# Rotary tables in 64 rows of 1 KB through ScalarE's DMA ring, and the last slab stored whole

## The chip, the cores and the metric

One core of a Trainium2 chip. The metric is the device time of one execution in microseconds (us); lower is better. A program on one core has no second die to compare with, so a run counts as fast unless it lies over 1.5% above the fastest of its kernel. Ratios and their 95% intervals are of the fast runs alone against the kernel before; they are not quite the ratios of the medians that stand beside them. A median and its range cover all runs, unless slow ones are named. "Span" is the length of the profiled execution, which is about 1.8 us shorter than the time measured for the same run.

## The reference

```python
batch, seq, dim, num_heads = 16, 512, 1024, 16        # head_dim 64, half_dim 32
x = x.reshape(batch, seq, num_heads, head_dim)        # float32
x1, x2 = x[..., :half_dim], x[..., half_dim:]
cos = cos[None, :, None, :]; sin = sin[None, :, None, :]   # each (seq, 32), float32
rotated = np.concatenate([x1 * cos - x2 * sin, x1 * sin + x2 * cos], axis=-1)
```

33.55 MB are read, 33.55 MB are written, and two tables of 64 KB, cos and sin, are shared by all batches and heads.

## The kernel before

Eight slabs of 4 MB (two batches each, one row of 32 KB per partition) go through five buffers. SyncE issues the loads, ScalarE the stores. The transfers that one of them issues stand in its own ring, a queue that sixteen DMA engines empty; the profile calls SyncE's ring q1 and ScalarE's q10. ScalarE casts a slab to bf16, VectorE multiplies twice and adds once, ScalarE casts back into the slab.

```python
load(0)
table = {}
raw = singles.tile([P, 2 * TR * half], f32, tag="raw")
for i, src in enumerate((cos, sin)):                       # 128 rows of 512 B each
    table[i] = nc.gpsimd.dma_start(out=view(raw, ...), in_=bass.AP(..., ap=[[TR * half, P], [1, TR * half]]))
for s in range(1, slots):                                  # loads 1 to 4 wait for the cos table
    tc.add_manual_dep(load(s).ins, table[0].ins.name, ...)
# ... four affine_selects build 0/1/-1 matrices "pick"; one cast raw -> tab1 (bf16)
# ... eight matmuls spread the table rows to the partitions of a slab: acc
tab = singles.tile([P, 2 * rpp * hd], bf16, tag="tab")
nc.vector.tensor_copy(out=tab, in_=acc)
# ... slabs 0, 6 and 7 in two half passes, the others in one
    back = nc.scalar.copy(out=xs, in_=xu)
    if s == nslabs - 1:                                    # last slab: each half stored by itself
        # ... second half's cast ordered behind the first half's issue
        part = nc.scalar.dma_start(out=dram(out_flat, s, r * dim, n * dim), in_=xs)
    elif r + n == rpp:
        nc.scalar.dma_start(out=dram(out_flat, s), in_=slab[s])
        if s + slots < nslabs:
            load(s + slots)
```

Each transfer issued by SyncE or ScalarE takes the next of eight semaphores in turn, and waits until the previous user of that semaphore has landed. At the end SyncE checks all semaphores, two by two, in a fixed order.

## Time and profile before

| | before |
|---|---|
| time, median of the runs beside the changed kernel | 162.49 us (162.31 to 162.63, 4 runs) |
| span of the profiled run | 160.43 us |
| first packet of the DMA engines; end of the last | 1.76; 158.97 us |
| load 0, sin table, load 1 landed | 13.40; 10.97; 23.11 us |
| store 0 issued; last store issued | 37.20; 145.13 us |

One "packet" is what a DMA engine moves in one turn: here a whole 32 KB row in 1.213 us. After the rows of a transfer each engine sends one more packet of 4 bytes, which counts its semaphore up (a semaphore packet). "Landed" is the time at which the semaphore has its full count. Packets and landings are read from the trace's records; the lines of the profile that carry the argument are in the prediction.

### The profile page before, as it was taken

The page shows a single profiled execution, that of the slowest core. Times are in us where ns is not written, and L with a number is a line of the kernel's source. Part 1 is how long each engine was busy: PE and PEld are TensorE (multiplying, and loading weights), DVE is VectorE, ACT ScalarE, POOL GpSimd, SP SyncE. Part 2 cuts the span into 40 slices and gives each one's busy share as a digit, 9 for nine tenths or more (in the row PEclk, how much of TensorE's full clock was granted, in tenths as well). Part 3 has the DMA queues.
Part 4 walks back from the last instruction along what each step waited for, and adds up shares of the span by engine and source line. Part 5 has one row for each costly group of instructions (what it writes and reads, how often), then busy time and mean ns, then how long its engine had stood idle before and what let it go on. Part 6 is the DMA issues. An engine that isn't in the chain of part 4 may idle for free.

```text
span 160.4 us, 169 instructions
## 1 busy us (share of the span) xinstructions
PE 1.0 (1%) x8; PEld 0.8 (1%) x8; DVE 108.5 (68%) x34; ACT 113.5 (71%) x23; POOL 3.4 (2%) x12
## 2 busy tenths in 40 slices
PE   0011000000000000000000000000000000000000
PEld 0010000000000000000000000000000000000000
DVE  0003799999989979997996099939649599920000
ACT  3006939998998999899907997099995999471000
POOL 7000000000000000000000000000000000000000
DMA  7999999999999999999999999999999999999994
GB/s 229 441 409 400 474 433 392 449 466 392 392 392 449 466 392 425 490 392 409 490 409 409 482 417 392 490 425 392 458 458 392 433 482 392 417 490 400 400 437 208
DMA packets 2512, 67.24 MB, mean 419 GB/s; under 512 B 304, under 2 KB 304, under 8 KB 336
## 3 DMA queue, kind: packets, MB, share of 16 engines
q1 hardware_dynamic: 1152, 33.55, 49.4%
q10 hardware_dynamic: 1296, 33.56, 48.5%
q0 software_dynamic: 64, 0.13, 0.2%
HBM read 33.69 MB, written 33.55 MB: 419 GB/s over the span
## 4 chain that ended last, share of the span: by engine, by line
DMA 59%; ACT 17%; issue 9%; DVE 4%; SPq 0%; POOLq 0%
DMA slab<-in_x_dram 40%; DMA out_dram<-slab 15%; ACT slab L146 11%; ACT xb L119 6%; DMA raw<-in_cos_dram 4%; DVE xb L143 1%; DVE xb L140 1%; DVE slab L140 1%; SPq L62 0%; POOLq L177 0%
## 5 line engine op out<-in xcount | busy, mean ns | idle before, releaser
L119 ACT CAST xb<-slab 128x4096 bf16<-128x4096 f32 (+1 forms) x11 | 56.6, 5155 | 27.4 <-DMA slab<-in_x_dram 26.1
L146 ACT CAST slab<-xb 128x4096 f32<-128x4096 bf16 (+1 forms) x11 | 56.6, 5153 | 3.4 <-DVE xb L143 3.4
L140 DVE TENSOR_TENSOR slab<-xb,tab 128x4096 bf16<-128x4096 bf16 (+1 forms) x11 | 35.9, 3260 | 19.7 <-ACT xb L119 19.6
L143 DVE TENSOR_TENSOR xb<-xb,slab 128x4096 bf16<-128x4096 bf16 (+1 forms) x11 | 35.9, 3261 | 0.3
L140 DVE TENSOR_TENSOR xb<-xb,tab 128x4096 bf16<-128x4096 bf16 (+1 forms) x11 | 35.9, 3260 | 0.3
L110 DVE CAST tab<-acc 128x1024 bf16<-128x1024 f32 x1 | 1.2, 1225 | 12.6 <-PE acc L104 12.6
L119 ACT ACT_TABLE_LOAD x1 | 1.3, 1283 | 0.7 <-PEq L177 0.7
L104 PE MATMUL acc<-tab,pick 128*128 128x128 bf16 x8 | 1.0, 305 | 11.6 <-POOL tab L98 11.6
L92 POOL TENSOR_SCALAR_AFFINE_SELECT pick<-pick 128x128 bf16<-128x128 bf16 x4 | 1.0, 289 | 0.1
L104 PEld LDWEIGHTS <-pick 128*128 128x128 bf16 x8 | 0.8, 136 | 11.4 <-issue 8.1
L73 POOL DMA_DIRECT2D raw<-in_cos_dram x1 | 0.7, 677 | 0.8 <-POOLq L177 0.8
L98 POOL CAST tab<-raw 128x256 bf16<-128x256 f32 x1 | 0.4, 398 | 7.0 <-DMA raw<-in_sin_dram 7.0
L89 POOL MEMSET pick<- 128x512 bf16 x1 | 0.5, 544 | 0.0
L73 POOL DMA_DIRECT2D raw<-in_sin_dram x1 | 0.5, 537 | 0.0
L177 POOL MEMSET const-float32-0.0<- 128x1 f32 x1 | 0.1, 99 | 0.2 <-issue 0.2
L177 POOL MEMSET const-bfloat16-1.0<- 128x1 bf16 x1 | 0.1, 102 | 0.0
L177 POOL MEMSET const-uint8-127<- 128x1 uint8 x1 | 0.1, 102 | 0.0
L177 POOL MEMSET const-float32-1.0<- 128x1 f32 x1 | 0.1, 99 | 0.0
## 6 DMA issues: line engine op xcount, KB each, us to landing
slab<-in_x_dram SPq DMA_DIRECT2D x8, 4096.0 KB, 24.6
out_dram<-slab ACTq DMA_DIRECT2D x7, 4096.0 KB, 27.8
out_dram<-slab ACTq DMA_DIRECT2D x2, 2048.0 KB, 15.3
raw<-in_cos_dram POOLq DMA_DIRECT2D x1, 64.0 KB, 7.1
raw<-in_sin_dram POOLq DMA_DIRECT2D x1, 64.0 KB, 9.1
```

The costliest lines, as they stand in the source:

```text
L73: table[i] = nc.gpsimd.dma_start(out=view(raw, i * TR * half, (1, TR * half)), in_=bass.AP(tensor=src.tensor, offset=src.offset, ap=[[TR * ...
L89: nc.gpsimd.memset(pick, 0.0)
L92: nc.gpsimd.affine_select(out=part, in_=part, compare_op=mybir.AluOpType.not_equal, fill=1.0 if g < G else -1.0, base=-(g % G), pattern=[[ ...
L98: nc.gpsimd.tensor_copy(out=tab1, in_=raw)
L104: nc.tensor.matmul(view(acc, (i * rpp + g * TR) * hd + h * half, (hd, TR), (1, half)), view(pick, (i * h * G + g) * P, (1, P)), view(tab1, ...
L110: nc.vector.tensor_copy(out=tab, in_=acc)
L119: nc.scalar.copy(out=view(xb[s], r * dim, (1, n * dim)), in_=view(slab[s], r * dim, (1, n * dim)))
L140: nc.vector.tensor_mul(out=t, in0=xu, in1=view(tab, a + r * hd, (hd, n), (0, nh), (1, hd)))
L143: nc.vector.tensor_add(out=xu, in0=xu, in1=view(t2, half, (hd, n * nh), (-half, 2), (1, half)))
L146: back = nc.scalar.copy(out=xs, in_=xu)
L177: nc = _bacc.Bacc("TRN2", target_bir_lowering=False, num_devices=1)
```

## The change

Its intent: get the tables off GpSimd's software queue and drop the loads' wait for them, halve the matmuls and selections, and save one store and its ordering.

```diff
-    raw = singles.tile([P, 2 * TR * half], f32, tag="raw")
-    ... two nc.gpsimd.dma_start of 128 rows of 512 B
-    for s in range(1, slots):
-        tc.add_manual_dep(load(s).ins, table[0].ins.name, ...)
+    cos_sb = singles.tile([SP, TW], f32, tag="cos_sb")        # SP = 64 rows of TW = 256 floats
+    sin_sb = singles.tile([SP, TW], f32, tag="sin_sb")
+    for t, src in ((cos_sb, cos), (sin_sb, sin)):
+        nc.scalar.dma_start(out=t, in_=bass.AP(..., ap=[[TW, SP], [1, TW]]))
+    for s in range(1, slots):
+        load(s)
     ... two affine_selects on 64 partitions instead of four on 128; two casts instead of one
-            for g in range(G):                                # eight matmuls of 128 columns
+            nc.tensor.matmul(...)                             # four of 256
-        back = nc.scalar.copy(out=xs, in_=xu)
-        if s == nslabs - 1:
-            ... part = nc.scalar.dma_start(... half ...)
-        elif r + n == rpp:
+        nc.scalar.copy(out=xs, in_=xu)
+        if r + n == rpp:
             nc.scalar.dma_start(out=dram(out_flat, s), in_=slab[s])
```

More of the change, by code (lines that the diff above doesn't have):

```diff
@@ L65 @@
     load(0)
-    TR = seq // P
-    G = rpp // TR
-    table = {}
-    raw = singles.tile([P, 2 * TR * half], f32, tag="raw")
-    for i, src in enumerate((cos, sin)):
-        table[i] = nc.gpsimd.dma_start(out=view(raw, i * TR * half, (1, TR * half)), in_=bass.AP(
-            tensor=src.tensor, offset=src.offset,
-            ap=[[TR * half, P], [1, TR * half]]))
-    for s in range(1, slots):
-        tc.add_manual_dep(
-            load(s).ins, table[0].ins.name,
-            mybir.DependencyInfo(mybir.DependencyClass.Sync,
-                                 mybir.DependencyReason.DATA),
-            reason="issue")
-    pick = singles.tile([P, 2 * G * P], bf16, tag="pick")
+    cos_sb = singles.tile([SP, TW], f32, tag="cos_sb")
+    sin_sb = singles.tile([SP, TW], f32, tag="sin_sb")
+    for t, src in ((cos_sb, cos), (sin_sb, sin)):
+        nc.scalar.dma_start(out=t, in_=bass.AP(
+            tensor=src.tensor, offset=src.offset, ap=[[TW, SP], [1, TW]]))
+    for s in range(1, slots):
+        load(s)
+    pick = singles.tile([SP, 2 * P], bf16, tag="pick")
     nc.gpsimd.memset(pick, 0.0)
-    for g in range(2 * G):
+    for g in range(2):
         part = view(pick, g * P, (SP, P // SP), (1, SP))
@@ L93 @@
             out=part, in_=part, compare_op=mybir.AluOpType.not_equal,
-            fill=1.0 if g < G else -1.0, base=-(g % G),
-            pattern=[[0, P // SP], [-G, SP]], channel_multiplier=1)
-    tab1 = singles.tile([P, 2 * TR * half], bf16, tag="tab1")
-    nc.gpsimd.tensor_copy(out=tab1, in_=raw)
+            fill=1.0 - 2.0 * g, base=0, pattern=[[0, P // SP], [-1, SP]],
+            channel_multiplier=1)
+    tab1 = singles.tile([SP, 2 * TW], bf16, tag="tab1")
+    for i, t in enumerate((cos_sb, sin_sb)):
+        nc.gpsimd.tensor_copy(out=view(tab1, i * TW, (1, TW)), in_=t)
     acc = psum.tile([P, 2 * rpp * hd], f32, tag="acc")
@@ L102 @@
         for h in range(2):
-            for g in range(G):
-                nc.tensor.matmul(
-                    view(acc, (i * rpp + g * TR) * hd + h * half, (hd, TR), (1, half)),
-                    view(pick, (i * h * G + g) * P, (1, P)),
-                    view(tab1, i * TR * half, (half, TR), (1, half)),
-                    start=True, stop=True)
+            nc.tensor.matmul(
+                view(acc, i * rpp * hd + h * half, (hd, rpp), (1, half)),
+                view(pick, i * h * P, (1, P)),
+                view(tab1, i * TW, (half, rpp), (1, half)),
+                start=True, stop=True)
     tab = singles.tile([P, 2 * rpp * hd], bf16, tag="tab")
@@ L144 @@
             out=xu, in0=xu, in1=view(t2, half, (hd, n * nh), (-half, 2), (1, half)))
-        back = nc.scalar.copy(out=xs, in_=xu)
-        if s == nslabs - 1:
-            if r > 0:
-                tc.add_manual_dep(
-                    back.ins, part.ins.name,
-                    mybir.DependencyInfo(mybir.DependencyClass.NoSync,
-                                         mybir.DependencyReason.DATA),
-                    reason="issue")
-            part = nc.scalar.dma_start(
-                out=dram(out_flat, s, r * dim, n * dim), in_=xs)
-        elif r + n == rpp:
+        nc.scalar.copy(out=xs, in_=xu)
+        if r + n == rpp:
             nc.scalar.dma_start(out=dram(out_flat, s), in_=slab[s])
```

## The prediction

> **What bounds the kernel now.** I read the page first: the busy slices and the DMA part.
>
> ```profile
> span 160.4 us, 169 instructions
> ...
> DVE  0003799999989979997996099939649599920000
> ACT  3006939998998999899907997099995999471000
> ...
> DMA  7999999999999999999999999999999999999994
> ...
> q1 hardware_dynamic: 1152, 33.55, 49.4%
> q10 hardware_dynamic: 1296, 33.56, 48.5%
> q0 software_dynamic: 64, 0.13, 0.2%
> ```
>
> VectorE and ScalarE have holes throughout; the DMA row has none between its first and its last slice. The three queues are SyncE's loads (q1), ScalarE's stores (q10) and GpSimd's two tables (q0). Their packets fill 49.4 + 48.5 + 0.2 = 98.1% of sixteen engines' span, 157.4 of 160.4 us, so at most 3.0 us of the span have an engine without a packet. The trace's packet records place them: the engines' first packets start between 1.76 and 2.60 us, the last ends at 158.97 us, and in between no engine pauses for more than 0.1 us. One packet is a 32 KB row and takes 1.213 us in the median; an engine has 8 loads and 8 stores of 8 rows each, 128 rows, 128 x 1.213 = 155.3 us. This is the bound: it can be beaten only by fewer bytes, faster packets, an earlier first packet or a shorter tail.
>
> Next the chain of waits in order of time, because it seems to say something else:
>
> ```profile
> 1.24 7.10 DMA raw<-in_cos_dram
> 8.33 0.02 issue
> 8.35 14.76 DMA slab<-in_x_dram
> 23.11 0.02 issue
> 23.14 3.00 ACT xb L119
> ```
>
> The end is followed back through the wait of loads 1 to 4 for the cos table: 7.10 us that the change removes. The reader might book them as a gain. But load 0 lands only at 13.40 us, so SyncE's ring still held rows of load 0 when the other loads were issued at 8.35. Busy time by stretches shows it (columns: stretch, length, busy PE, PEld, DVE, ACT, POOL, clock, DMA share, GB/s):
>
> ```profile
> 2.00:8.35 6.35, 0.00 (x0) 0.10 (x1) 0.00 (x0) 0.01 (x1) 2.01 (x6) 1.00 0.86 361
> 8.35:13.40 5.05, 1.01 (x8) 0.74 (x7) 0.80 (x1) 0.00 (x0) 0.40 (x1) 1.00 1.00 428
> ```
>
> The share in a stretch counts a packet where it starts; the 0.86 is the first row of each engine, which began just before 2.00 and took 1.5 to 2.3 us, not idleness. At 8.35 nothing had run dry: share 1.00 to 13.40.
>
> Last the timeline of the start and of the end, for the slack of the compute chain:
>
> ```profile
> 11.10 0.40 POOL L98 CAST tab<-raw 128x256 bf16<-128x256 f32 x1 [7.02 <-DMA raw<-in_sin_dram]
> ...
> 12.60 1.23 DVE L110 CAST tab<-acc 128x1024 bf16<-128x1024 f32 x1 [12.60 <-PE acc L104]
> 13.43 7.11 ACT L119 CAST xb<-slab 128x4096 bf16<-128x4096 f32 x2 [11.41 <-DMA slab<-in_x_dram]
> 17.06 2.29 DVE L140 TENSOR_TENSOR slab<-xb,tab 128x4096 bf16<-128x4096 bf16 x1 [3.24 <-ACT xb L119]
> ...
> 28.32 2.29 DVE L143 TENSOR_TENSOR xb<-xb,slab 128x4096 bf16<-128x4096 bf16 x1
> 30.06 7.11 ACT L146 CAST slab<-xb 128x4096 f32<-128x4096 bf16 x2
> ```
>
> And of the end:
>
> ```profile
> 138.12 0.34 ACTq L155 DMA_DIRECT2D out_dram<-slab  x1
> ...
> 145.13 0.34 ACTq L155 DMA_DIRECT2D out_dram<-slab  x1
> ```
>
> The finished table stands at 12.60 + 1.23 = 13.83 us, yet VectorE starts at 17.06: it waits for ScalarE's cast of the first half slab, which waits for load 0. And the last store is issued at 145.13, while the span ends at 160.4: over 15 us in which only DMA works.
>
> **What the Trainium skill says.** "DMA: Bandwidth & Descriptors", section "Queues, rings and completion order", says that each DMA engine goes round the queues that have work and changes only at packet boundaries. This trace agrees: while q0 had table packets, each engine put one 1.213 us row of q1 between two turns of q0. The same page, section "Issuing engines are not separate DMA queues", says that the issuing engine does not matter to bandwidth, only to its sequencer's time; here an issue took 0.34 us on ScalarE, 0.33 to 0.46 on SyncE, and 0.68 and 0.54 on GpSimd. Section "Where 436 GB/s comes from" derives a ceiling of 435.2 GB/s; 16 rows of 32,768 B in 1.213 us are 432 GB/s, so faster packets are not to be expected. "SBUF — State Buffer", section "Door 1: The DMA port swizzle", says that a tile on partitions 0 to 63 reaches only half of the write ports; here that concerns two tables of 64 KB among 33.69 MB read, so I leave it out, and no run so far shows it.
>
> **The change part by part.**
>
> (1) Wait of loads 1 to 4 on the table: removed. They will be queued behind load 0 by about 0.74 + 5 x 0.4 = 2.7 us instead of 10.1 us. Rows within the ring stay in order, load 0 first. Gain: 0, since the ring was never empty.
>
> (2) Tables by ScalarE's ring. Before, q0 had 64 packets: per engine and table one of 4,096 B (eight 512 B pieces, 159 ns) and one semaphore packet (9 ns), so 2 x 168 ns = 0.34 us of an engine. After, 64 rows of 1 KB over 16 engines are 4 rows per engine and table. If ScalarE's ring sends each as its own packet, as it does with 32 KB rows, that is 8 rows and 2 semaphores per engine; I estimate 50 ns for a row (a quarter of 159 ns and something for a packet): 8 x 50 + 2 x 9 = 0.42 us. Cost of the DMA engines: +0.1 us.
>
> (3) The tables come later. Ten turns per engine instead of four, a q1 row between each. When does a new ring get its first turn? q0's first packet started at 6.0 us, four to five us after its issue; the first store, issued at 37.20, got its first packet at 42.24, 5.0 us later, behind about four rows of q1. I choose the same for the tables: issue at 0.75, first turn at about 6.0. From there nine more turns have nine packets of q1 between them; one is load 0's semaphore packet, so eight rows: 6.0 + 8 x 1.213 + 0.5 = 16.2 us on the typical engine, 16.5 on the last, against 10.97 before. cos needs five turns: 6.0 + 4 x 1.27 = about 11.1. If the table rows go in with the first rows of load 0 instead, sin lands near 14.
>
> (4) From sin's landing to the table: the cast of 64x256 as long as that of 128x256, 0.40; of four matmuls (256 columns instead of 128, half as many as before) only the two of sin are still to come, about 0.5; eviction of the same 128x1024, 1.23; semaphores 0.2. 16.5 + 2.3 = 18.8 us. VectorE's first multiply moves from 17.06 to 18.8, by 1.7 us. Before, it was hidden behind load 0 with 3.2 us to spare; now it is the table that VectorE waits for.
>
> (5) What those 1.7 us cost. Slab 0's last addition ends at 28.32 + 2.29 = 30.61; ScalarE wants it at 30.06 + 3.55 = 33.6, because its cast of slab 1 waits for load 1 (23.11). Slack 3.0 us, so store 0 is still issued at 37.2. Slab 1's last addition (39.45 + 4.43 = 43.88 in the timeline) has 0.66 us before ScalarE wants it (44.54), so store 1 goes out 1.0 us late, at 52.6; but ScalarE's ring is busy with store 0 until 61.25, and store 1 has 9 us of slack. ScalarE has 4.88 us idle before 85.14, which absorb the rest. DMA: 0.
>
> (6) GpSimd: the memset and two selections instead of four, on 64 partitions, and no DMA issue. All done by 4 us then as now, waiting for sin. 0.
>
> (7) The last store whole. Its first half was issued at 138.12; now all goes at 145.13. At that time ScalarE's ring holds store 6, whose rows end at 148.74 us in the packet records. Load 0 shows that an empty ring starts 1.0 us after the issue, so the whole store is in the ring at about 146.2, 2.5 us before it is needed. Then 8 rows of 1.213 = 9.70 us against 16 half rows of 0.611 = 9.78. -0.1 us.
>
> Sum: 0 + 0.1 + 0 - 0.1 = 0 us.
>
> **The rivals.** First: the 7.10 us of the chain are real and come off, 155.5 us. For it speaks only the chain; against it the full DMA row and the 1.00 share between 8.35 and 13.40. Hardly possible, since 155.3 us of rows remain, with 1.8 us before them.
> Second: the late table delays the first store and the whole chain behind it, by 1.7 us or more: 164.3. For it: VectorE's wait does change hands. Against it: the slack of 3.0 us, and five slabs of buffers: with all loads queued, DMA has read work to about 52 us without a single store. If ScalarE's ring had to stand behind all five loads the tables would come at about 50 us, and VectorE's start and with it store 0 would move from 37.2 to some 74, and about 20 us without DMA would follow; but the first store began 5.0 us after its issue with q1 still full, and then took turns one to one.
> Third: a hole before the last store. It opens only if the last cast slips by over 2.5 us, through a later load 7 (now 123.85); then each further us costs one: 163 to 165.
> Fourth: a small gain. On q10's first use, at 40.3 to 42.6 us, each engine's row of q1 took 1.6 to 2.1 instead of 1.213 us, 0.65 us more. If that is the price of a ring's first use, the tables now pay it inside the slow first rows, and up to 0.6 us come off: 161.9.
>
> **Range and chances.** The three runs before lie within 0.23 us. The sum is 0, with the fourth rival a little likelier than the third: 162.4 us, 161.6 to 163.3 for 8 in 10. Within 2% means 159.3 to 165.8: 0.96. Faster 0.01, as the rows leave no room; slower 0.03, for tables stuck behind the loads.
>
> **What would show it.** Right: DMA shares of the queues near 98% again; loads 1 to 4 issued by 3 us without moving load 1's landing from 23.1; sin landing at 14 to 17, VectorE's first wait ended by the table; store 0 still at 37.2; last issue at 145 with 15 us to the end; GpSimd's queue gone. Wrong: a slice of the DMA row below 9 inside, sin landing after 20, store 0 after 38, or rows slower than 1.213 us.

## More of the kernel before

One view that the prediction did not use becomes important later: SyncE's own waits (what waited, on whom, us in total, times, longest).

```profile
SPq L62 <- DMA out_dram<-slab: 87.8, 3, 51.1
SPq L191 <- DMA out_dram<-slab: 35.4, 1, 35.4
...
SPq L62 <- DMA raw<-in_cos_dram: 7.2, 1, 7.2
```

L62 is the load: three loads wait for stores to free a buffer, and load 1 waits 7.2 us for the cos table. L191 is the end of the program. There a single check waits for a store, the last one; no later check has anything left to wait for, but each still takes its time.

## The result, and the profile after

The changed kernel took 161.99 us (161.92 to 162.55, 4 runs) against 162.49; the ratio is 0.9979, 95% interval 0.9960 to 0.9998. It is the same within 2%, with a gain of 0.03 to 0.65 us that just clears the noise. The spans of its four runs are 160.2, 160.1, 160.8 and 160.2 us.

The page of the changed kernel, to be laid beside the lines in the prediction:

```profile
span 160.2 us, 157 instructions
...
DMA  7999999999999999999999999999999999999993
...
q1 hardware_dynamic: 1152, 33.55, 49.3%
q10 hardware_dynamic: 1312, 33.69, 48.8%
```

The DMA row is as full as before, the queues fill 49.3 + 48.8 = 98.1% of the span as before, and GpSimd's queue is gone. That is why a change with so many parts moves so little; e2_tables and e3_free below take the parts alone.

The start of its timeline, and its last store (start, length, engine and line, what):

```profile
0.74 2.50 SPq L62 DMA_DIRECT2D slab<-in_x_dram  x5
0.75 0.54 ACTq L71 DMA_DIRECT2D cos_sb<-in_cos_dram  x1
...
1.32 0.61 ACTq L71 DMA_DIRECT2D sin_sb<-in_sin_dram  x1
...
17.59 0.39 POOL L90 CAST tab<-sin_sb 64x256 bf16<-64x256 f32 x1 [4.91 <-DMA sin_sb<-in_sin_dram]
...
18.65 1.22 DVE L101 CAST tab<-acc 128x1024 bf16<-128x1024 f32 x1 [18.65 <-PE acc L95]
19.97 2.29 DVE L131 TENSOR_TENSOR slab<-xb,tab 128x4096 bf16<-128x4096 bf16 x1
...
31.23 2.29 DVE L134 TENSOR_TENSOR xb<-xb,slab 128x4096 bf16<-128x4096 bf16 x1
...
37.70 0.35 ACTq L139 DMA_DIRECT2D out_dram<-slab  x1
...
144.28 0.34 ACTq L139 DMA_DIRECT2D out_dram<-slab  x1
```

All five loads are issued by 3.2 us instead of 10.1, yet load 1 landed at 23.61 us, half a us later than before. The tables come later, not earlier: sin landed at 17.54 us against 10.97. VectorE starts at 19.97 instead of 17.06, with no idle time between the table and its first multiply, so the table is now what it waits for. Its last addition for slab 0 ends at 33.52, still before ScalarE wants it (30.56 + 3.55 = 34.11), so store 0 goes out at 37.70; the 0.5 us against before are load 1's.

The chain of waits (start, length, what) looks quite different:

```profile
0.75 11.49 DMA cos_sb<-in_cos_dram
...
19.97 2.30 DVE slab L131
...
68.21 30.49 DMA out_dram<-slab
98.70 0.02 SPq L62
98.72 0.04 issue
98.76 24.18 DMA slab<-in_x_dram
```

Before, it ran through the cos table, load 1, store 0, load 5 and load 7; now it runs through the table and VectorE's first slabs to store 2 and load 7. A new 11.49 us wait for a table stands on it, and the time did not grow. A chain shows one path back from the last instruction that ended on an engine; here, with the DMA engines full all the time, the waits on it were exchanged without any effect on the end.

### The profile page after: what moved, and what is told of

It is laid out like the page before. It is cut to its first block, busy times and chain, and to the rows that moved or that the text cites. A ratio compares the mean times of both kernels' runs of the same rounds, so it can differ in the third digit from the quotient of the medians.

```text
span 160.2 us, 157 instructions
## 1 busy us (share of the span) xinstructions
PE 1.2 (1%) x4; PEld 0.5 (0%) x4; DVE 108.4 (68%) x34; ACT 113.6 (71%) x23; POOL 1.8 (1%) x9
## 3 DMA queue, kind: packets, MB, share of 16 engines
q1 hardware_dynamic: 1152, 33.55, 49.3%
q10 hardware_dynamic: 1312, 33.69, 48.8%
## 4 chain that ended last, share of the span: by engine, by line
DMA 41%; ACT 21%; DVE 20%; issue 6%; PE 0%; POOLq 0%; POOL 0%; ACTq 0%; DVEq 0%; SPq 0%
DMA out_dram<-slab 19%; DMA slab<-in_x_dram 15%; ACT slab L137 13%; ACT xb L110 8%; DMA cos_sb<-in_cos_dram 7%; DVE xb L131 7%; DVE slab L131 7%; DVE xb L134 6%; DVE tab L101 1%; PE acc L95 0%; POOLq L172 0%; POOL tab L90 0%; ACTq L139 0%; DVEq L131 0%; SPq L62 0%
## 5 line engine op out<-in xcount | busy, mean ns | idle before, releaser
L95 PE MATMUL acc<-tab,pick 64*128 64x256 bf16 x4 | 1.2, 392 | 17.5 <-POOL tab L90 17.5
L83 POOL TENSOR_SCALAR_AFFINE_SELECT pick<-pick 64x128 bf16<-64x128 bf16 x2 | 0.5, 287 | 0.1
L95 PEld LDWEIGHTS <-pick 64*128 64x128 bf16 x4 | 0.5, 113 | 17.7 <-issue 16.2
## 6 DMA issues: line engine op xcount, KB each, us to landing
sin_sb<-in_sin_dram ACTq DMA_DIRECT2D x1, 64.0 KB, 16.2
```

The source lines that it names most:

```text
L83: nc.gpsimd.affine_select(out=part, in_=part, compare_op=mybir.AluOpType.not_equal, fill=1.0 - 2.0 * g, base=0, pattern=[[0, P // SP], [-1 ...
L95: nc.tensor.matmul(view(acc, i * rpp * hd + h * half, (hd, rpp), (1, half)), view(pick, i * h * P, (1, P)), view(tab1, i * TW, (half, rpp) ...
```

## The experiments

Twelve kernels ran, all correct. The theory at the start: only DMA time counts, and the small gain is a row of the loads that is no longer stretched. In the kernel before, the last row of each engine ahead of the first store (at 40.3 us) took 1.56 to 2.13 instead of 1.213 us, 0.66 us per engine; in the changed kernel that is gone, while 80 rows beside the table packets took 1.27 to 1.36 us, 0.42 us per engine. The rivals: the gain is the tail's, or the removed wait's.

### Each part by itself

**e1_whole**: only the last store whole.

```diff
 kernel before
-        if s == nslabs - 1:
-            ... each half stored by itself
-        elif r + n == rpp:
+        if r + n == rpp:
```

> The kernel before with only the last store whole. My theory (the store ring is never empty before the end, so how the last slab is cut doesn't matter): the same time as before, within 0.2 us (162.3 to 162.6), the last packet ends near 158.9 us, and the rows of q1 at 40 us are stretched by 0.65 us as before. Rival (the 0.5 us gained come from the tail: fewer packets and no second issue): near 162.0, and the last packet ends 0.3 us or more earlier.

162.13 us (161.96 to 162.35, 5 runs) beside 162.39 of before: ratio 0.9982 (0.9970 to 0.9995). My theory fails: this part alone brings a gain of 0.29 us, about as large as the whole change's 0.34. The stretched rows at 40 us are still there (0.85 us per engine). But the rival's second half fails too: the last packet does not end earlier (159.15 us against 158.97). What this trace gains over before lies after its last packet: 1.20 us to the end of the span against 1.45.

**e2_tables**: the other parts without that one.

```diff
 changed kernel
-        if r + n == rpp:
+        if s == nslabs - 1:
+            ... each half stored by itself
+        elif r + n == rpp:
```

> The changed kernel with the last store in two halves again, so only the tables by ScalarE's ring and the loads without a wait. My theory (the gain is the stretched row at the first use of ScalarE's ring, 0.65 us, less 0.4 us that rows lose beside the table packets): the whole of the gain, near 162.0 to 162.2, no stretched row at 40 us, 80 or so stretched rows between 8 and 16 us. Rival (the tail): 162.5.

162.30 us (162.25 to 162.77, 5 runs), ratio 1.0000 (0.9988 to 1.0012). Tables and free loads bring nothing measurable, although the stretch at 40 us shrank to 0.12 us per engine in this trace and 96 rows beside the tables lengthened as expected. The stretched row is not the gain.

**e3_free**: the loads without their wait, tables still by GpSimd.

```diff
 kernel before
-        tc.add_manual_dep(load(s).ins, table[0].ins.name, ...)
+        load(s)
```

> The kernel before, its loads 1 to 4 not waiting for the cos table any more, tables still by GpSimd. My theory: nothing, 162.4 to 162.6, because the load ring was not empty when they were issued. Rival (the 7.10 us of the chain of waits are real): 155.5; a weaker one (earlier descriptors fill the ring better): 162.0.

162.45 us (162.38 to 164.37, 6 runs), ratio 1.0022 (0.9989 to 1.0056). Of the 7.10 us on the chain of waits the interval leaves at most 0.2 us to gain.

**e4_warm**: an early use of ScalarE's ring.

```diff
 kernel before
     load(0)
+    warm = singles.tile([16, 128], f32, tag="warm")
+    nc.scalar.dma_start(out=warm, in_=bass.AP(tensor=cos.tensor, offset=cos.offset, ap=[[128, 16], [1, 128]]))
```

> The kernel before with one 8 KB load more, 16 rows of 512 B, in ScalarE's ring right after load 0; nobody reads it. My theory (each engine's row of q1 at 40 us is stretched because ScalarE's ring is used for the first time, whatever it moves): no stretched row at 40 us, at most a few short ones near 6 us, busy time per engine down by 0.5 to 0.65 us, time 161.8 to 162.0, so the extra load makes the kernel faster. Rival (the stretch belongs to the first store, the turn from reading to writing): 162.5, the stretch still there at 40 us.

162.51 us (162.38 to 162.72, 5 runs), ratio 1.0006 (0.9994 to 1.0018), and the stretch stands at 40 us as before (0.84 us per engine). "A ring's first use costs it" is refuted. What causes the stretch stays open: it appeared in all traces with GpSimd's tables, was small or absent in most of those with the tables in ScalarE's ring, and still stood, 0.56 us, in one of these (e10_rows below).

### What happens after the last packet

The records of SyncE's last instructions show it. After the last landing SyncE finishes its checks, 0.062 us apart, and then all engines meet twice and the semaphores are cleared. Semaphores are dealt out in turn, so the number of transfers decides where the last store's semaphore stands in the order of checks. SyncE's waits in e1_whole:

```profile
SPq L181 <- DMA out_dram<-slab: 36.0, 4, 9.6
```

Before, one long check caught the last store first, and four more checks came after its landing. Here four checks wait for the last four stores one by one, 9.6 us each at the longest, and the last store's is the last: nothing is left to check when it lands. Four checks of 0.062 are 0.25 us; from the last landing to the end it is 0.88 us here against 1.11. To test this I shifted the turn with transfers that nobody reads.

**e12_one**: whole store as in e1_whole, and one 64-byte load more.

```diff
 e1_whole
+    nop = singles.tile([1, 16], f32, tag="nop0", name="nop")
+    nc.sync.dma_start(out=nop, in_=bass.AP(tensor=cos.tensor, offset=cos.offset, ap=[[16, 1], [1, 16]]))
```

> The kernel before with the last store whole (which alone took 0.3 us off) and one 64-byte load more, which shifts the semaphores back, so that the last store's is again followed by four checks. My theory: from the last landing to the end 1.1 us again instead of 0.88, and the gain of the whole store shrinks to its packets, 0.05 us: 162.3 to 162.45, as before. Rival: the gain stays, 162.1.

162.34 us (162.19 to 162.66, 5 runs), ratio 0.9998 (0.9985 to 1.0010). The gain is gone, as the theory has it (though its interval overlaps that of e1_whole), and SyncE's waits have their old form:

```profile
SPq L186 <- DMA out_dram<-slab: 54.8, 1, 54.8
```

**e11_seven**: the reverse, two halves and seven loads more.

```diff
 kernel before
+    for k in range(7):                       # behind load 4, in SyncE's ring
+        nop = singles.tile([1, 16], f32, tag=f"nop{k}", name="nop")
+        nc.sync.dma_start(out=nop, ...)      # 64 bytes, as above
```

> The kernel before, its last store in two halves, with seven 64-byte loads more in SyncE's ring behind load 4; nobody reads them. They shift the round of eight DMA semaphores, so that the last store's semaphore is the last that SyncE checks at the end, not the first of the remaining five pairs. My theory (0.25 us of the gain is this order of checks, which the whole store happens to change): from the last landing to the end of the span 0.88 us instead of 1.11, time 0.15 to 0.25 us below before, about 162.2, although it does more. Rival (the whole store itself, its larger packets, brings the gain): not faster than before, 162.4 to 162.7.

166.10 us (165.53 to 167.41, 6 runs), ratio 1.023 (1.0201 to 1.0258). The edit broke something else. The small loads queued behind load 4 and landed only at about 62 us; store 1 needed the semaphore of one of them and went out at 62.35 us instead of 51.59, and the DMA engines ran dry (1.4 us per engine of holes, and 1.9 us of longer rows after 60 us). From the last packet's end to the end of the span it took 1.23 us, as expected, but the time says nothing about it.

**e14_six**: the same for the changed kernel, six loads.

```diff
 changed kernel
+    for k in range(6):                       # behind load 4, in SyncE's ring
+        ... the same 64-byte load
```

> The changed kernel with six 64-byte loads in SyncE's ring behind load 4, to bring the last store's semaphore to the last check there too. My theory: from the last landing to the end 0.8 to 0.9 us instead of 1.00, time 0.1 to 0.2 us below the changed kernel: 161.8 to 161.9, faster than both. Rival: no gain over the changed kernel, 162.0 to 162.2.

164.84 us (163.81 to 164.91 in 4 fast runs; two slow ones at 167.13 and 167.44), ratio 1.0123 (1.0101 to 1.0145). A related fault: the six loads move store 1 on to the semaphore of load 4 itself, which landed at 65.44 us, so store 1 went out at 65.52 us (in the trace, which fell into a slow run, so I take no more from it).

**e15_first7**: seven small loads where they hold up no store. (They do hold up the issue of loads 2 to 4, to 13.4 us and later; load 2 landed at 32.79 us, before at 32.83.)

```diff
 kernel before
+    for k in range(7):                       # the first of all, in ScalarE's ring
+        nop = singles.tile([1, 16], f32, tag=f"nop{k}", name="nop")
+        nc.scalar.dma_start(out=nop, ...)
     load(0)
```

> The kernel before, its last store in two halves, with seven 64-byte loads more, this time the first of all in ScalarE's ring, where no later transfer has to wait long for their semaphores (the earlier version held up store 1, issued at 62.35 instead of 51.6 us). The last half's semaphore is again the last that SyncE checks. My theory: from the last packet's end to the end of the span 1.20 to 1.25 us instead of 1.45, so 0.1 to 0.2 us faster than before with the same two halves: 162.2 to 162.4. Rival (the whole store's larger packets gain the 0.3 us): not faster, 162.4 to 162.7.

162.18 us (162.14 to 162.31, 4 runs) beside 162.40, ratio 0.9988 (0.9973 to 1.0002). With the two halves kept and seven transfers more, it is 0.2 us faster, in size as expected; but the interval includes 1, so the time alone does not show it. SyncE's waits:

```profile
SPq L196 <- DMA out_dram<-slab: 36.1, 5, 9.6
```

Five waits for stores, one after the other, so again the last check is the last store's. The traces of fast runs that bear on it, from the records:

| kernel | last store | checks after its landing | last packet's end, span | difference, us |
|---|---|---|---|---|
| before | halves | 4 | 158.97, 160.43 | 1.45 |
| e12_one | whole | 4 | 158.97, 160.42 | 1.45 |
| e1_whole | whole | 0 | 159.15, 160.35 | 1.20 |
| e15_first7 | halves | 0 | 159.15, 160.38 | 1.22 |
| e2_tables | halves | 4 | 159.60, 160.98 | 1.38 |
| changed kernel | whole | 3 | 158.87, 160.21 | 1.34 |

In the first four rows the difference follows the number of checks and not the form of the store: four checks are 0.23 us with the halves and 0.24 us with the whole store. The other fast traces fit: e4_warm, with one transfer more than before, has 5 checks and 1.50 us; e3_free 4 and 1.45; e11_seven none and 1.23; e7_late1, e9_tail and e10_rows 3 and 1.33 to 1.34. Clearing the semaphores took 0.139 us with GpSimd's tables and 0.096 to 0.098 us without; with the changed kernel's one check less, that is most of what sets the last two rows apart from the first. So the traces show what the order of checks costs. That it makes up the timed gain of e1_whole (0.29 us, 0.08 to 0.49 by its interval) fits, but it is at the edge of the noise.

### How late the tables and the last store may come

**e7_late1**: the tables behind load 1.

```diff
 changed kernel
-    for t, src in ((cos_sb, cos), (sin_sb, sin)):
-        nc.scalar.dma_start(...)
-    for s in range(1, slots):
-        load(s)
+    load(1)
+    for t, src in ((cos_sb, cos), (sin_sb, sin)):
+        nc.sync.dma_start(...)
+    for s in range(2, slots):
+        load(s)
```

> The changed kernel with its tables in SyncE's ring behind load 1 instead of in ScalarE's, so they land at about 24 us instead of 17.5, and VectorE starts at about 26.4 instead of 20.0. Theory of the prediction (a late table costs nothing while loads are left): store 0 goes out at about 43.6 us instead of 37.7, the DMA engines stay full or lose about 1 us at 61 us when load 5 waits for store 0; 162 to 163. Rival (a late table moves everything behind it one to one): 168. It also shows what stretches a row of q1 at 40 us in the kernels with GpSimd's tables: if this kernel, with neither GpSimd's ring nor an early use of ScalarE's, has the stretch at its first store, an early and longer use of ScalarE's ring removes it; if not, GpSimd's ring causes it.

163.49 us (162.06 to 163.50 in 3 fast runs; a slow one at 165.00), ratio 1.0034 (1.0001 to 1.0067). Its timeline:

```profile
25.01 1.23 DVE L104 CAST tab<-acc 128x1024 bf16<-128x1024 f32 x1 [25.01 <-PE acc L98]
26.34 4.49 DVE L134 TENSOR_TENSOR slab<-xb,tab 128x4096 bf16<-128x4096 bf16 x2
...
44.67 0.38 ACTq L142 DMA_DIRECT2D out_dram<-slab  x1
```

VectorE starts 6.4 us later than in the changed kernel, store 0 goes out 7.0 us later, and the ratio puts the kernel 0.5 us above before: nowhere near one to one. It is not free either. SyncE's ring started no row between 54.6 and 66.6 us, because load 5 waits for store 0. The engines still had stores (holes of only 0.09 us each), but rows after 60 us lengthened by 1.13 us per engine. There was no stretch before the first store here, with neither GpSimd's ring nor an early use of ScalarE's, so an early use is not needed to remove it. But right behind the table packets, at 22.1 to 22.7 us, sixteen rows took 1.56 to 1.84 us, 0.43 us per engine: a stretch of the same kind in another place.

**e10_rows**: the old layout in the new ring.

```diff
 kernel before, last store whole, loads without their wait
-        table[i] = nc.gpsimd.dma_start(...)  # 128 rows of 512 B
+        table[i] = nc.scalar.dma_start(...)
```

> The changed kernel's ring and whole store, with the layout of before: each table in 128 rows of 512 B on 128 partitions, all through ScalarE's ring. It measures what the 64 rows of 1 KB do. My theory (one row is one packet and one turn beside a row of q1): 18 turns per engine instead of 10, sin lands at about 28 us instead of 17.5, VectorE starts at about 30.5, store 0 goes out at about 47.6; the loads end at about 52 us, so a hole of 1 to 3 us opens there or at 62 us: 163 to 165. Rival (the packets are packed as in GpSimd's queue, or the layout doesn't matter): sin by 18 us, 162.0.

163.40 us (162.65 to 164.81, 4 runs), ratio 1.0071 (1.0033 to 1.0108).

```profile
23.47 0.40 POOL L94 CAST tab<-raw 128x256 bf16<-128x256 f32 x1 [21.12 <-DMA raw<-in_sin_dram]
...
24.97 1.23 DVE L106 CAST tab<-acc 128x1024 bf16<-128x1024 f32 x1 [24.97 <-PE acc L100]
```

The records have 256 packets of 512 B, one for each row, so packets are not packed together in this ring, and sin landed at 23.34 us instead of 17.54. It came sooner than the 28 us I had worked out. Its first packet started at 3.57 us, not at 6, which is half of that; and the turns lay about 1.23 us apart, two of them only 0.28, instead of the 1.3 of the changed kernel. No row beside these packets lengthened, so the lengthening in the changed kernel goes with the new layout of 64 partitions and 1 KB rows; which of the two does it, no run shows. Store 0 went out at 43.57 us. The 64 rows of 1 KB thus matter: without them the new ring costs over a us.

**e16_first6**: the shifted checks for the changed kernel, better placed.

```diff
 changed kernel
+    for k in range(5):                       # the first of all, in ScalarE's ring
+        ... nc.scalar.dma_start(out=nop, ...)
     load(0)
     ...
+    nc.sync.dma_start(out=nop, ...)          # one more, behind load 4
```

> The changed kernel with six 64-byte loads more, five the first of all in ScalarE's ring and one in SyncE's behind load 4, to bring the last store's semaphore to the last check. The tables are issued about 1.8 us later, and should land at 19 to 20 us. My theory: from the last packet's end to the end 1.15 to 1.2 us instead of 1.34, store 0 at most 2 us later without effect, time 0.1 to 0.2 us under the changed kernel's: 161.8 to 162.0. Rival: no gain, 162.0 to 162.3.

165.83 us (165.01 to 166.50 in 5 fast runs; a slow one at 167.57), ratio 1.0206 (1.0182 to 1.0230). A miss of my own model: each small load is two packets (64 bytes and a semaphore) on one engine, each packet takes a turn beside a row of 1.213 us, so five of them are ten turns ahead of the tables on that engine. In its trace (a slow run) sin landed at 26.04 us, 8.5 us later, and store 0 was issued at 45.75. The step from the last packet's end to the end of the span was 1.16 us, but the kernel lost far more than it could gain: at 60 to 70 us alone the trace has 2.0 us of holes per engine.

**e9_tail**: the last two slabs in one pass each, so that the compute chain ends later.

```diff
 changed kernel
-        n = rpp if 1 <= s < nslabs - 2 else rpp // 2
+        n = rpp if 1 <= s else rpp // 2
```

> The changed kernel with slabs 6 and 7 in one pass each, not two halves, so that the compute chain ends later. It measures the margin of the last store. By the prediction the whole store may be issued until about 147.5 us at no cost, and then each us costs one. The last cast ends at about 123 + 7 + 13.3 + 7 = 150.3 us, the last store is issued there instead of at 144.3, ScalarE's ring has drained at about 148.7 to 149: a hole of about 3 us, 164.5 to 166. Rival (DMA time is all that counts, the issue's time does not): 162.0 to 162.3.

164.69 us (164.19 to 166.46, 4 runs), ratio 1.0159 (1.0117 to 1.0202). Its DMA row, and the busy time of the stretch from 148 to 155 us (the last two numbers are DMA share and GB/s):

```profile
DMA  7999989989999999999999999999999997992885
```

```profile
148.00:155.00 7.00, 0.00 (x0) 0.00 (x0) 0.00 (x0) 4.56 (x1) 0.00 (x0) 1.00 0.53 225
```

The last store was issued at 152.59 us and its first packet started at 153.4, while ScalarE's ring had drained at about 149.7. So the hole that the changed kernel avoids does open when the last store comes late: here it was 3.1 to 3.9 us on an engine, with 0.4 to 1.0 us more at 139, where store 6 came late too. This trace is of the slowest of the four runs; its span is 4.47 us longer than the changed kernel's, and its holes are about 4.4 us per engine. (The changed kernel had a DMA share of 0.98 from 143 to 150 us.)

No version beat both kernels clearly. The kernel before with only its last store whole (162.13 us) is as good as the changed one within the noise, and simpler.

## Why the prediction was right

The predicted 162.4 us and the range of 161.6 to 163.3 hold the measured 161.99. By its steps:

1. The removed wait was worth 0, as said: e3_free.
2. The tables' packets cost what was estimated: a 1 KB packet took 47 ns (estimate 50). That rows beside them would lengthen was not foreseen; it cost 0.42 us per engine in the trace, which e2_tables does not show as time. In the pair of traces the stretch at 40 us fell away at the same time, 0.66 us, so that the engines' busy time went from 157.3 to 157.0 us. That the sum stayed near zero is luck in part: the lengthened rows and the stretch (which only its fourth rival names) stood outside it and offset each other. Whether the 64 partitions lengthen the rows, which the prediction set aside, e10_rows leaves open.
3. Ten turns, the first at 6.06 us (6.0 foreseen), eight rows between: the semaphore packets ran at 16.50 to 17.09 us (16.2 to 16.5 foreseen). Because of the lengthened rows one step took 1.30, not 1.21, and the landing came 0.45 us after the last packet, so sin landed at 17.54. The first turn was luck in part: it rests on the 5.0 us of the first store before, which are 3.4 to 4.7 us in the other traces, and e10_rows had its first turn at 3.57, e15_first7 at 1.63 us.
4. From landing to VectorE's start 2.4 us (2.3 foreseen): 19.97 instead of 18.8.
5. Slack: store 0 was not held up by the table, and store 1 (53.86 us instead of 51.59; 52.6 foreseen) changed nothing. That loads cover a late table up to 52 us was too generous: e7_late1 and e10_rows pay 0.5 and 1.2 us by their ratios when store 0 goes out at about 44 us.
6. GpSimd: nothing on the path, as said.
7. The last store: issued at 144.28 us, before store 6's landing at 149.54, no hole. From its first row to its first semaphore packet 9.67 us, against 9.72 for the two halves: a gain of 0.05 us where 0.1 was foreseen. e9_tail shows that the margin is real and what it costs to overrun it.

Several signs that the prediction had set for being right were missed by about half a us (load 1 landed at 23.61, sin at 17.54, store 0 went out at 37.70), and one of those for being wrong did show: 80 rows slower than 1.213 us. The time came out all the same.

The second and third rivals did not come about, and the first fell with e3_free. The fourth rival, a gain from the first use of ScalarE's ring, had the right sign for the wrong reason: e4_warm refutes it. What was missing is a term for the end of the program: the checks after the last landing, 3 instead of 4, and a shorter clearing. In the profiled pair of 0.22 us in span, 0.12 us lie there (1.454 to 1.337) and 0.10 us in an earlier end of the last packet. The timed gain of 0.34 us by the ratio is larger than the 0.12; the rest is not settled. e2_tables differs from the changed kernel only in the halves and one check and lies 0.21% above it, with intervals of about 0.12 to 0.19% on either side, so I can't tell the rest from noise.

## What to carry to other kernels

When the DMA row is full from the first packet to the last and the queues' shares add up to nearly the whole span, read the slack of everything else and expect a change beside the transfers to move nothing, however long a wait it removes from the chain, as long as no ring runs dry (e9_tail, e11_seven) and store 0 is not much later (e7_late1, e10_rows). Small transfers placed in a ring beside large rows cost turns, not bytes (five loads of 64 bytes put sin 8.5 us later in e16_first6): count packets, and count who reuses their semaphores. When a difference is a few tenths of a us, look also at what the program does after its last packet: an unrelated change in the number of transfers can shift it.

## What the Trainium skill lacked or had wrong

- "DMA: Bandwidth & Descriptors", section "Queues, rings and completion order", gives 9 to 17 descriptors as typical for a packet. In ScalarE's ring each row was a packet of its own, 1 KB in 47 ns on average, 512 B in 28 ns (e10_rows), 32 KB in 1.213 us; only GpSimd's queue packed eight 512 B pieces into 4,096 B (159 ns).
- No page that I read says how long a ring waits for its first turn beside a full one: 5.0 us for the first store before but 3.4 to 4.7 in the other traces, 5.3 us for the tables but 2.8 in e10_rows, and 0.9 us for the first small load of e15_first7, issued together with load 0.
- No page has the lengthened rows: 1.27 to 1.36 us beside the 1 KB table packets (none beside the 512 B packets of e10_rows), 1.56 to 2.13 us just before the first store of the kernel before.
- "DMA: Bandwidth & Descriptors", section "Specifications", has about 358 GB/s as the HBM limit of one core; here one core moved 420 GB/s over the span, reading and writing. The row divides a stack's figure by two cores; the page's own measurement for one core while the other idles, 425 GB/s, is nearer.
- No page has the order in which a program checks its DMA semaphores at its end: 0.062 us for each check after the last landing, 0 to 5 of them.
